# 512-column values for heads 2 and 3, attentions queued ahead of their Q and K, longer holds, and another pace of the side sums

## The chip, the cores and the metric

The kernel runs on one core of a Trainium2 chip. TensorE (PE) does the matmuls, VectorE (DVE), ScalarE (ACT) and GpSimd (POOL) the elementwise work, SyncE (SP) issues the loads and stores. Each engine works through its own queue in order, and waits where an operand is not there yet. The metric is the time of one execution on the device in microseconds; a profiled execution gives a trace of what each engine did and waited for.

## The reference

One encoder layer on x of 1024 tokens by 1024 channels, in float32:

```python
h = rmsnorm(x, norm_mix)
q, k, v, r, lr_f, lr_b, u, g_a, g_b = split(h @ w_in)
log_a_f = log_sigmoid(lr_f @ w_decay_up_fwd + b_decay_fwd) / 16    # and log_a_b
# 4 heads, keys of 128, values of 256, in chunks of 64, forward and backward:
#   b = cumsum(log_a) within the chunk;  q_e = q exp(b);  k_e = k exp(-b)
#   scores = masked q_e k_e^T;  kv = k_d^T v;  state = decay * state + kv
#   o = scores v + q_e state
o = rms(o_fwd + o_bwd) per head * gla_norm * silu(r)
y_a = o @ w_branch_gla
y_b = (pooled mixer of u) @ w_pool_group * pool_scale
x = x + (sigmoid(g_a) * y_a + sigmoid(g_b) * y_b) @ w_out
x = x + (silu(gate) * up) @ w_ffn_out      # of rmsnorm(x) @ w_ffn_in
out = rmsnorm(x, norm_final)
```

What the change touches is the first projection, q, k and v of the four heads, and the attention that follows for each head.

## The kernel before

Every float32 operand of a product is split in two parts, a rounded one and the rest (`split_to`: ScalarE copies, VectorE or POOL subtracts), and one product is three matmuls: high by high, high by low, low by high (`products`). `mm3` is one such product; a bank of PSUM holds 512 columns of float32, and eight products over the 1024 channels (KT = 8 blocks of 128) fill it. Weights come by `load` as raw tiles (four buffers), which `Weights.split` turns into wh and wl (ScalarE casts, POOL subtracts; six buffers each).

The program writes the order of all engines itself (a manual schedule). The stream of projection products on TensorE sets the pace. After each product, `pump` counts its width in units of 512 columns and lets other work have its turn: `pending` (splits of the next weights, one for each two units), `aside` (sums that are prepared for later stages: branch sums of the GLA output weight, wsum tiles on POOL; later feature sums on VectorE and POOL; each step followed by a number of units, the pace), and `side`. In `side` stand the attentions, Python generators that are run one after the other: each issues some steps, then yields the number of units until its next ones. So the work of one head's attention is spread among the projection products of the next head.

An attention begins with four decay stages (two halves of the tokens, two directions; names by tile): z, a matmul for the decay's logits, la and z on VectorE and ScalarE (abs, exp, ln), a scan on VectorE with tot and z behind it, the exponentials on ScalarE (qe, z, fac), then ke on VectorE, qe and fac on POOL. HOLD is the number of units between one of these stages and the next. The transposed keys follow (kp on TensorE, kt on ScalarE and VectorE), then seven state steps for the backward direction: kv on TensorE, st on VectorE, sb and so on ScalarE, where so is what the next st adds to. Then the scores (sc on TensorE, masked on VectorE, split into p), and for each block of tokens the output op. When the head is done, its o is normalised on VectorE (`unscaled`, run by the next attention behind its z stage) and stored by SP (o_out).

The main loop does Q and K of a head (`project_qk`, each two banks of 512 tokens), and then begins the head's attention. Values of heads 0 and 1 are made at once, 512 columns a bank (`pair_products`, in the stage of head 0). Those of heads 2 and 3 are made by head: `values` fills 256 columns of a bank for each of eight blocks of tokens, from weights that `Weights` splits.

Of the kernel before, what the change touches and what calls it, by code (L numbers as in the profile page):

```python
# [10 lines left out]
F32 = mybir.dt.float32  # L11
F32R = mybir.dt.float32r
# [41 lines left out]
def kernel(  # L54
# [42 lines left out]
    def slot(dtype=F32, shape=(2, HALF), s="slot"):  # L97
        return slots.tile([P, *shape], dtype, tag="slot", name=name(s))
# [10 lines left out]
    def bank(pool, s="ps"):  # L109
        return pool.tile([P, HALF], F32, tag=pool.name, name=name(s))  # L110
# [88 lines left out]
    def split_to(hi, lo, src, eng=nc.vector):  # L199
        nc.scalar.copy(hi, src)  # L200
        eng.tensor_tensor(lo, src, as_f32(hi), op=ALU.subtract)  # L201
# [92 lines left out]
    def tokens(pair, t):  # L294
        return tuple(p[:, (t % 4) * P : (t % 4 + 1) * P] for p in pair)
# [138 lines left out]
    def low_rank_weights():  # L434
# [7 lines left out]
    def value_slots():  # L442
        return [(slot(F32R, (4, DV), "vh"), slot(F32R, (4, DV), "vl")) for _ in range(2)]

    cols = const.tile([P, 40], F32, tag="cols", name="cols")

# [41 lines left out]
    split_pair_weight()  # L488
    for kp in range(2):
        transpose_tile(trs[kp], xn[1], 1, kp)  # L490
    pair_v = [[], []]

    def pair_products(ts, before=None):
        banks = [bank(ps_mm) for _ in ts]
        for k in range(KT):
            if before:
                before(k)
            for ps, t in zip(banks, ts):
                mm3(ps[:, :], tokens(hT(k, t // 4), t), pair_w[k], k == 0, k == KT - 1)
        for ps, t in zip(banks, ts):  # L500
            for h in range(2):
                if t // 4 == len(pair_v[h]):
                    pair_v[h].append((slot(F32R, (4, DV), "vh"), slot(F32R, (4, DV), "vl")))
            parts = [[part[:, t % 4, :] for part in v[t // 4]] for v in pair_v]
            halves = [ps[:, h * DV : (h + 1) * DV] for h in range(2)]
            for (hi, _), src in zip(parts, halves):
                nc.scalar.copy(hi, src)
            for (hi, lo), src in zip(parts, halves):
                nc.vector.tensor_tensor(lo, src, as_f32(hi), op=ALU.subtract)

    def first_steps(k):
        if k == 2:
# [211 lines left out]
            aside.pop(0)  # L724


    v_heads, o_heads, unscaled = {}, {}, []
    HOLD, SCORES = 4.4, 6

    def project_qk():  # L730
# [7 lines left out]
        return q, k  # L738

    def attention(h, q, k):  # L740


        qe, ke = {}, {}
# [139 lines left out]
        kts[0, 1] = transposed_keys(0, 1)  # L883
        exponentials(1, 0)
        yield 2.5
        while h not in v_heads:
            yield 0.5
        v = v_heads[h]

        def value(n):  # L890
            return tuple(part[:, n % 4, :] for part in v[n // 4])
# [12 lines left out]
        p = scores(0)  # L904
        yield SCORES
        o = [slot(shape=(4, DV), s="o") for _ in range(2)]
        ms = vec(NT, "oms")
        old = sf = None
# [50 lines left out]
    def first_qk():  # L959
        q, k = slot(s="q"), slot(s="k")  # L960
        low_rank(0)
        weights = [take()]
        for half in range(2):
            if half:
                finish_side()
                low_rank(1)
                prepare()
            for n, (dst, scale) in enumerate(((q, DK**-0.5), (k, 1.0))):
                if n == len(weights):
                    weights.append(take(ahead=False))  # L970
                ps = feature_major(weights[n], hT, half)
                nc.scalar.activation(dst[:, half, :], ps[:, :], AF.Copy, scale=scale)
        return q, k

    for h in range(HEADS):
        qk = project_qk() if h else first_qk()
        begin(attention(h, *qk))
        if h == 0:
            for ts in ((7,), (6,), (5, 4)):
                pair_products(ts)  # L980
            v_heads.update(enumerate(pair_v))
            prepare_beside(map(branch_jobs, range(4)), 5)
        if h > 1:
            v = value_slots()
            w = take()
            for t in range(NT):
                values(w, v, t)
            v_heads[h] = v

    class Unit:  # L990

# [131 lines left out]
    for j in range(KT):  # L1123
        if 2 <= j <= 4:
            load_o(j - 2)
        w = take()
        if j == 6:
            for _ in range(2):
                gunits[0].load()
        if j == 7:  # L1130
            gates_ahead.step()
        if j < BY:
            whole_r = slot(s="r")
        for half in range(2):
# [898 lines left out]
```

## Time and profile before

| | before |
|---|---|
| time, median of 3 runs | 1379.94 us (1379.63 to 1380.65) |
| profiled execution | 1380.1 us |
| its span, first to last instruction | 1378.1 us |
| granted TensorE clock | 0.999 |
| busy TensorE / weight loads | 1367.6 us (99%) / 1147.4 us (83%) |
| busy VectorE / ScalarE / POOL | 61% / 47% / 54% |
| value matmuls of heads 2 and 3 | 384 of 128x256 |

Names in the rows are tiles, out<-in, with buffer numbers left out; L274 is the line of `products`, so that nearly all projection and state matmuls stand on one line and are told apart by tiles: ps for a projection bank, kv, op, sc and kp for an attention. Matmuls overlap, and the duration of one says how long it was on its way; how many microseconds it takes of TensorE is seen from the distance between two starts. What stands in brackets is the idle time of the engine before the instruction and what ended it.

The attention of head 1 (counted from 0) lies beside Q and K of head 2 and the values of head 2, from about 132 us in the span on; that of head 2 beside Q and K of head 3 and its values, that of head 3 beside the R columns.

### The profile page before, as it was taken

How to read it: one execution, taken by the hardware profiler on the slowest of the kernel's cores; microseconds unless marked ns; L12 is line 12 of the kernel's file. 1: busy time of each engine (PE TensorE's matmuls, PEld its weight loads, DVE VectorE, ACT ScalarE, POOL GpSimd, SP SyncE). 2: the span in 40 equal slices, each digit the busy share in tenths (PEclk: the TensorE clock that was granted, in tenths of full speed). 3: DMA queues.
4: the chain of work that ended last, by engine and by line, in shares of the span. 5: the costliest groups of instructions: out<-in, count | busy, mean ns of one | idle time of the engine just before them, and what ended most of it. 6: DMA issues, size and time to landing. Idle time of an engine off the chain costs nothing. (4 is left out here: it accounts for less than half of the span.)

```text
span 1378.1 us, 18207 instructions
## 1 busy us (share of the span) xinstructions
PE 1367.6 (99%) x6514; PEld 1147.4 (83%) x6514; DVE 839.8 (61%) x1027; ACT 642.6 (47%) x1170; POOL 750.7 (54%) x554
## 2 busy tenths in 40 slices
PE   9999999999999999999999999999999999999998
PEld 7888899988888888888888888888888888888886
DVE  6364656557745876688883955656656556343375
ACT  7375666655334445554347533333333334444353
POOL 3222617132297646668665276666666667455454
PEclk9999999999999999999999999999999999999999
DMA  6121413312478678996516355555544447985561
GB/s 226 31 62 47 147 62 125 110 48 77 138 230 278 197 229 277 371 394 216 175 61 245 115 176 176 176 176 176 165 143 139 144 136 266 385 306 186 170 214 77
DMA packets 166586, 243.60 MB, mean 177 GB/s; under 512 B 10936, under 2 KB 95968, under 8 KB 166496
## 3 DMA queue, kind: packets, MB, share of 16 engines
q1 hardware_dynamic: 166352, 242.18, 52.3%
q8 instruction: 51, 0.84, 0.3%
q14 instruction: 39, 0.32, 0.1%
q10 hardware_dynamic: 144, 0.26, 0.1%
HBM read 164.55 MB, written 77.86 MB: 176 GB/s over the span
## 5 line engine op out<-in xcount | busy, mean ns | idle before, releaser
L201 POOL TENSOR_TENSOR wl<-fs,wh 128x512 fp32r<-128x512 f32 x120 | 167.6, 1400 | 157.2 <-ACT wh L200 103.2
L274 PE MATMUL ps<-gh,wh 128*128 128x512 f32 x616 | 240.9, 391 | 0.0
L274 PE MATMUL ps<-gl,wh 128*128 128x512 f32 x616 | 240.2, 390 | 0.3 <-DVE gl L1591 0.3
L274 PE MATMUL ps<-gh,wl 128*128 128x512 f32 x616 | 240.0, 390 | 0.0
L201 POOL TENSOR_TENSOR wl<-fraw,wh 128x512 fp32r<-128x512 f32 x90 | 129.7, 1441 | 63.6 <-ACT wh L200 61.2
L274 PE MATMUL ps<-hh,wh 128*128 128x512 f32 x376 | 151.9, 404 | 0.0
L201 POOL TENSOR_TENSOR ol<-gor,oh 128x1024 fp32r<-128x1024 f32 (+1 forms) x42 | 101.7, 2425 | 85.7 <-ACT oh L200 59.6
L274 PE MATMUL ps<-hh,wl 128*128 128x512 f32 x376 | 146.9, 391 | 0.0
L274 PE MATMUL ps<-hl,wh 128*128 128x512 f32 x376 | 146.8, 390 | 0.0
L274 PEld LDWEIGHTS ps<-gl,wh 128*128 128x128 f32 x616 | 115.8, 188 | 24.1 <-DVE gl L1591 0.7
L274 PEld LDWEIGHTS ps<-gh,wh 128*128 128x128 f32 x616 | 115.8, 188 | 24.0 <-ACT hb L1610 0.3
L274 PEld LDWEIGHTS ps<-gh,wl 128*128 128x128 f32 x616 | 115.7, 188 | 24.1
L201 POOL TENSOR_TENSOR wl<-raw,wh 128x512 fp32r<-128x512 f32 x40 | 54.7, 1379 | 121.9 <-ACT wh L200 103.5
L274 PE MATMUL ps<-oh,oh 128*128 128x512 f32 x308 | 120.0, 390 | 0.0
L274 PE MATMUL ps<-oh,ol 128*128 128x512 f32 x308 | 120.0, 390 | 0.0
L274 PE MATMUL ps<-ol,oh 128*128 128x512 f32 x308 | 120.0, 389 | 0.0
L201 POOL TENSOR_TENSOR wl<-wraw,wh 128x512 fp32r<-128x512 f32 x56 | 92.2, 1675 | 44.7 <-ACT wh L200 44.5
L201 DVE TENSOR_TENSOR ol<-wor,oh 128x1024 fp32r<-128x1024 f32 (+1 forms) x42 | 62.8, 1506 | 68.1 <-ACT oh L200 55.5
L200 ACT CAST wh<-fs 128x512 fp32r<-128x512 f32 x120 | 73.8, 615 | 26.1 <-DVE fs L1010 25.1
L274 PEld LDWEIGHTS ps<-hh,wl 128*128 128x128 f32 x376 | 70.6, 188 | 15.0
L274 PEld LDWEIGHTS ps<-hl,wh 128*128 128x128 f32 x376 | 70.9, 188 | 12.9
L274 PEld LDWEIGHTS ps<-hh,wh 128*128 128x128 f32 x376 | 70.8, 188 | 12.8
(279 smaller groups left out, 3126.3 us busy)
## 6 DMA issues: line engine op xcount, KB each, us to landing
fraw<-in_w_ffn_in_dram SPq DMA_DIRECT2D x44, 512.0 KB, 7.2
gor<-g_out SPq DMA_DIRECT2D x35, 512.0 KB, 5.8
g_out<-s SPq DMA_DIRECT2D x44, 256.0 KB, 2.3
raw<-in_w_in_dram SPq DMA_DIRECT2D x40, 256.0 KB, 5.1
fraw<-in_w_in_dram SPq DMA_DIRECT2D x20, 512.0 KB, 7.1
wor<-t_out SPq DMA_DIRECT2D x20, 512.0 KB, 4.5
g_out<-g SPq DMA_DIRECT2D x33, 256.0 KB, 2.5
x<-in_x_dram SPq DMA_DIRECT2D x16, 512.0 KB, 4.5
```

The lines of the kernel that those rows point to most:

```text
L200: nc.scalar.copy(hi, src)
L201: eng.tensor_tensor(lo, src, as_f32(hi), op=ALU.subtract)
L274: nc.tensor.matmul(ps, a[i], b[j], start=first and n == 0, stop=last and n == 2, skip_group_check=onto)
```

## The change

Five things are changed.

1. The values of heads 2 and 3 are made together, 512 columns a bank, in one stage behind Q and K of head 2, by a new class `ValueWeights`. It loads the eight weight blocks of 128 rows by 512 columns, takes them in the order 0, 1, 6, 7, 2, 3, 4, 5 (6 and 7 into slots of their own), and does the token blocks 7 and 6 first, in two banks: the first six weights for both, then the last two for both. Then come blocks 5 to 0. `values` and `value_slots` go; the splitting of a bank into both heads is shared with heads 0 and 1 (`keep_values`). Q and K of head 3 come behind it.
2. The attention of head h + 1 is put into `side` before its Q and K are projected. It begins when the one before has ended, and waits (in steps of half a unit) for `qk_heads` where it first needs q and k, and before each state step for the value tile of that step.
3. HOLD goes from 4.4 to 5.0.
4. A step of the branch sums is followed by 4.5 units and not 5.
5. A step of the feature sums is followed by 2.8 units and not 2.3.

```diff
-        cols_of = [(Q0 + h * DK, DK), (K0 + h * DK, DK), (V0 + h * DV, DV)]
-        order += [(w_in, KT, *c) for c in cols_of[: 2 if h < 2 else 3]]
+        order += [(w_in, KT, c + h * DK, DK) for c in (Q0, K0)]
...
-    def values(w, v, t):
-        ps = bank(ps_mm)
-        for kt in range(KT):
-            mm3(ps[:, :DV], tokens(hT(kt, t // 4), t), w(kt), kt == 0, kt == KT - 1)
-        split_to(*(part[:, t % 4, :] for part in v[t // 4]), ps[:, :DV])
...
+    def keep_values(heads, t, ps):
+        vs = [v_slots[h] for h in heads]
+        for v in vs:
+            if t // 4 not in v:
+                v[t // 4] = slot(F32R, (4, DV), "vh"), slot(F32R, (4, DV), "vl")
+        parts = [[part[:, t % 4, :] for part in v[t // 4]] for v in vs]
+        for h in heads:
+            v_tiles[h].add(t)
+        halves = [ps[:, h * DV : (h + 1) * DV] for h in range(2)]
+        for (hi, _), src in zip(parts, halves):
+            nc.scalar.copy(hi, src)
+        for (hi, lo), src in zip(parts, halves):
+            nc.vector.tensor_tensor(lo, src, as_f32(hi), op=ALU.subtract)
...
-            prepare_beside(map(branch_jobs, range(4)), 5)
-        if h > 1:
-            v = value_slots()
-            w = take()
-            for t in range(NT):
-                values(w, v, t)
-            v_heads[h] = v
+            prepare_beside(map(branch_jobs, range(4)), 4.5)
+        if h == 2:
+            value_weights.pop().products()
...
-    HOLD, SCORES = 4.4, 6
+    HOLD, SCORES = 5.0, 6
...
+    class ValueWeights:
+        ORDER = (0, 1, 6, 7, 2, 3, 4, 5)
+        IN_SLOTS = (6, 7)
...
+        def load(self, upto):
+            while len(self.raw) < min(upto, KT):
+                k = self.ORDER[len(self.raw)]
+                raw = wts.tile([P, HALF], F32, tag="raw", name=name("raw"), bufs=4)
+                nc.sync.dma_start(raw[:, :], w_in[k * P : (k + 1) * P, V0 + 2 * DV : V0 + 4 * DV])
+                self.raw.append(raw)
...
+                    mm3(banks[t][:, :], tokens(hT(k, t // 4), t), self.parts[k], at == 0, at == KT - 1)
+                if ks[-1] == self.ORDER[-1]:
+                    keep_values((2, 3), t, banks[t])
+
+            early, late = self.ORDER[:6], self.ORDER[6:]
+            for ks in (early, late):
+                for t in (7, 6):
+                    steps(t, ks)
+            for t in reversed(range(NT - 2)):
+                if t == 2:
+                    fetch()
+                steps(t, self.ORDER)
...
+        while h not in qk_heads:
+            yield 0.5
+        q, k = qk_heads[h]
         apply_decay(1, 1)
...
+            while n not in v_tiles[h]:
+                yield 0.5
             old = advance(old, n, 1, kts[n // 4, 1], sb[m // 4][:, m % 4, :], m == 0)
...
-        qk = project_qk() if h else first_qk()
-        begin(attention(h, *qk))
+        if h:
+            project_qk(h, h == 2)
+        else:
+            first_qk()
+            begin(attention(0))
+        if h < HEADS - 1:
+            begin(attention(h + 1))
...
-                prepare_beside([feature_jobs(0), feature_jobs(1)], 2.3)
+                prepare_beside([feature_jobs(0), feature_jobs(1)], 2.8)
```

On TensorE, where the values of head 2 began before (ps_1633 is their bank; hh and hl are parts of h, kp and kv belong to the attention of head 1):

```order
L274 MATMUL ps_1633<-wh_1518,hh_223 128x256
L274 MATMUL ps_1633<-wl_1519,hh_223 128x256
L274 MATMUL ps_1633<-wh_1518,hl_224 128x256
L826 MATMUL kp_1637<-ident,ke_1584 128x128 x4
L274 MATMUL ps_1633<-wh_1518,hh_223 128x256
L274 MATMUL ps_1633<-wl_1519,hh_223 128x256
L274 MATMUL ps_1633<-wh_1518,hl_224 128x256
```

and the same place now, where ps_1650 is a bank for both heads:

```order
L273 MATMUL ps_1650<-wh_1466,hh_494 128x512
L273 MATMUL ps_1650<-wl_1467,hh_494 128x512
L273 MATMUL ps_1650<-wh_1466,hl_495 128x512
L885 MATMUL kp_1654<-ident,ke_1596 128x128 x4
L273 MATMUL ps_1650<-wh_1480,hh_494 128x512
L273 MATMUL ps_1650<-wl_1481,hh_494 128x512
L273 MATMUL ps_1650<-wh_1480,hl_495 128x512
```

Matmuls of 256 columns became matmuls of twice the width, and the transposes kp of head 1's attention stand at the same place in the stage.

On SP's queue, before, the store of head 0's normalised output (o_out) and the loads of the value weights of head 2 (raw_1497 to raw_1503) behind it; wsum and s_out are loads and stores of the branch sums:

```order
L687 DMA s_out_542<-wsum_1051 128x512
L604 DMA wsum_1452<-in_w_branch_gla_dram 128x2x512
L604 DMA wsum_1453<-in_w_branch_gla_dram 128x2x512
L570 DMA o_out_561<-o_1164 128x1024
L570 DMA o_out_561<-o_1165 128x1024
L687 DMA s_out_541<-wsum_1050 128x512
L208 DMA raw_1497<-in_w_in_dram 128x2x256
L208 DMA raw_1499<-in_w_in_dram 128x2x256
L208 DMA raw_1501<-in_w_in_dram 128x2x256
L208 DMA raw_1503<-in_w_in_dram 128x2x256
```

and now (the raw tiles are the value weights of both heads, one block of 128 rows each):

```order
L738 DMA raw_1397<-in_w_in_dram 128x512
L738 DMA raw_1399<-in_w_in_dram 128x512
L563 DMA o_out_561<-o_1177 128x1024
L563 DMA o_out_561<-o_1178 128x1024
L738 DMA raw_1462<-in_w_in_dram 128x512
L738 DMA raw_1464<-in_w_in_dram 128x512
L738 DMA raw_1478<-in_w_in_dram 128x512
L738 DMA raw_1490<-in_w_in_dram 128x512
L738 DMA raw_1501<-in_w_in_dram 128x512
L680 DMA s_out_542<-wsum_1028 128x512
L597 DMA wsum_1506<-in_w_branch_gla_dram 128x2x512
L597 DMA wsum_1507<-in_w_branch_gla_dram 128x2x512
```

Two of the value weights are now loaded ahead of o_out and five directly behind it; the second pair of wsum loads moved from ahead of o_out to behind them.

On ScalarE, the casts of the value weights and the first exponentials of head 1's decays (qe, z and fac), before:

```order
L737 ACTIVATE q_1379<-ps_1385 128x512
L764 ACT_TABLE_LOAD
L764 ACTIVATE z_1389<-z_1389 128x512
L764 ACTIVATE z_1397<-z_1397 128x512
L764 ACTIVATE z_1405<-z_1405 128x512
L764 ACTIVATE z_1417<-z_1417 128x512
L737 ACTIVATE q_1379<-ps_1458 128x512
L200 CAST wh_1518<-raw_1497 128x512
L798 ACT_TABLE_LOAD
L798 ACTIVATE qe_1522<-z_1389 128x512
```

and now:

```order
L823 ACTIVATE z_1413<-z_1413 128x512
L200 CAST wh_1466<-raw_1397 128x512
L796 ACTIVATE q_1391<-ps_1401 128x512
L200 CAST wh_1480<-raw_1399 128x512
L200 CAST wv_1492<-raw_1462 128x512
L200 CAST wv_1503<-raw_1464 128x512
L796 ACTIVATE q_1391<-ps_1471 128x512
L200 CAST wh_1535<-raw_1478 128x512
L857 ACT_TABLE_LOAD
L857 ACTIVATE qe_1542<-z_1372 128x512
```

Before, one cast of a value weight loaded behind o_out stood ahead of the exponentials; now there are three of them (raw_1462, raw_1464, raw_1478), and two of weights loaded earlier.

More of the change, by code (lines that the diff above doesn't have):

```diff
@@ L440, in low_rank_weights @@
         nc.vector.tensor_tensor(up[32:64], uraw[32:64], as_f32(up[32:64]), op=ALU.subtract)
-    def value_slots():
-        return [(slot(F32R, (4, DV), "vh"), slot(F32R, (4, DV), "vl")) for _ in range(2)]
     cols = const.tile([P, 40], F32, tag="cols", name="cols")
@@ L490 @@
         transpose_tile(trs[kp], xn[1], 1, kp)
-    pair_v = [[], []]
+    v_slots, v_tiles, qk_heads = [{} for _ in range(HEADS)], [set() for _ in range(HEADS)], {}
+    def keep_values(heads, t, ps):
[11 more added lines that the diff above has]
+            nc.vector.tensor_tensor(lo, src, as_f32(hi), op=ALU.subtract)
     def pair_products(ts, before=None):
@@ L500, in pair_products @@
         for ps, t in zip(banks, ts):
[L501 to L509, printed above, removed]
+            keep_values((0, 1), t, ps)
     def first_steps(k):
@@ L724, in finish_beside, with __init__, split, splits @@
             aside.pop(0)
-    v_heads, o_heads, unscaled = {}, {}, []
-    HOLD, SCORES = 4.4, 6
-    def project_qk():
+    o_heads, unscaled = {}, []
+    HOLD, SCORES = 5.0, 6
+    class ValueWeights:
+        ORDER = (0, 1, 6, 7, 2, 3, 4, 5)
+        IN_SLOTS = (6, 7)
+        def __init__(self):
+            self.raw, self.parts = [], {}
+            self.load(2)
+            self.splits(4)
+        def load(self, upto):
[4 more added lines that the diff above has]
+                self.raw.append(raw)
+        def split(self):
+            n = len(self.parts)
+            self.load(n + 4)
+            k = self.ORDER[n]
+            if k in self.IN_SLOTS:
+                w = slot(F32R, s="wv")
+                parts = w[:, 0, :], w[:, 1, :]
+            else:
+                parts = [wts.tile([P, HALF], F32R, tag=s, name=name(s))[:, :] for s in ("wh", "wl")]
+            split_to(*parts, self.raw[n][:, :], nc.gpsimd)
+            self.parts[k] = parts
+        def splits(self, n):
+            pending.extend([self.split] * n)
+        def products(self):
+            while pending:
+                pending.pop(0)()
+            banks = {}
+            self.split()
+            self.split()
+            def steps(t, ks):
+                if t not in banks:
+                    banks[t] = bank(ps_mm)
+                for k in ks:
+                    if (t, k) == (0, 6):
+                        prepare()
+                        credit[0] = 1.0
+                    at = self.ORDER.index(k)
+                    mm3(banks[t][:, :], tokens(hT(k, t // 4), t), self.parts[k], at == 0, at == KT - 1)
[9 more added lines that the diff above has]
+                steps(t, self.ORDER)
+    def project_qk(h, last=False):
         q = slot(s="q")
@@ L733, in project_qk @@
         for dst, scale in ((q, DK**-0.5), (k, 1.0)):
-            w = take()
+            final = last and dst is k
+            w = take(not final)
+            if final:
+                value_weights[0].splits(2)
+            elif last:
+                value_weights.append(ValueWeights())
             for half in range(2):
@@ L737, in project_qk, with attention @@
                 nc.scalar.activation(dst[:, half, :], ps[:, :], AF.Copy, scale=scale)
-        return q, k
-    def attention(h, q, k):
+        qk_heads[h] = q, k
+    def attention(h):
         qe, ke = {}, {}
@@ L885, in attention @@
         yield 2.5
-        while h not in v_heads:
-            yield 0.5
-        v = v_heads[h]
         def value(n):
-            return tuple(part[:, n % 4, :] for part in v[n // 4])
+            return tuple(part[:, n % 4, :] for part in v_slots[h][n // 4])
         sb = [slot(shape=(4, DV), s="sb") for _ in range(2)]
@@ L905, in attention @@
         yield SCORES
+        while 0 not in v_tiles[h]:
+            yield 0.5
         o = [slot(shape=(4, DV), s="o") for _ in range(2)]
```

6 lines of the change are left out of this document (3 added, 3 removed).

## The prediction

> **What bounds the kernel now.** I read the page's busy shares first, then the chain that ended last, then the groups of the value matmuls kept apart by shape.
>
> ```profile
> PE 1367.6 (99%) x6514; PEld 1147.4 (83%) x6514; DVE 839.8 (61%) x1027; ACT 642.6 (47%) x1170; POOL 750.7 (54%) x554
> PE 44%; DVE 1%; ACT 1%; issue 0%; POOLq 0%; POOL 0%; DVEq 0%; ACTq 0%
> L274 PE MATMUL ps<-wh,hh 128*128 128x256 f32 x128 | 40.0, 312 | 0.0
> L274 PE MATMUL ps<-wh,hl 128*128 128x256 f32 x128 | 36.2, 283 | 0.0
> L274 PE MATMUL ps<-wl,hh 128*128 128x256 f32 x128 | 36.2, 283 | 0.0
> ```
>
> TensorE is the bound; the rest of the chain is small. So the change is worth what it takes from TensorE's stream of matmuls and from the gaps in it. The last three rows are the 384 value matmuls of heads 2 and 3. Their mean is not what they cost: the busy column holds overlapping matmuls. The cost of one is its distance from the next, which the timeline of TensorE shows, first in a value stage (256 columns), then in a Q/K or R stage (512):
>
> ```profile
> 232.38 0.28 PE L274 MATMUL ps<-wh,hl 128*128 128x256 f32 x1
> ...
> 235.97 0.28 PE L274 MATMUL ps<-wh,hl 128*128 128x256 f32 x1
> 273.27 0.39 PE L274 MATMUL ps<-hh,wl 128*128 128x512 f32 x1
> ...
> 274.86 0.39 PE L274 MATMUL ps<-hh,wh 128*128 128x512 f32 x1
> ```
>
> There are 30 starts from the first row to the second: 3.59/30 = 0.120 us each. There are 7 from the third to the fourth: 1.59/7 = 0.227 us.
>
> The gaps come next. Here are TensorE's rows around the attention of head 1 (which runs in the value stage of head 2), with one row of head 3's:
>
> ```profile
> 154.53 0.28 PE L274 MATMUL ps<-wh,hl 128*128 128x256 f32 x1
> 155.29 0.66 PE L826 MATMUL kp<-ident,ke 128*128 128x128 f32 x4 [0.49 <-DVE ke L808]
> ...
> 157.58 0.28 PE L274 MATMUL kv<-vh,kt 128*128 128x256 f32 x1
> ...
> 168.82 1.16 PE L856 MATMUL sc<-qe,ke 128*128 128x128 f32 x8 [0.24 <-DVE st L840]
> ...
> 175.08 0.39 PE L274 MATMUL op<-vh,p 128*128 128x256 f32 x1 [0.22 <-DVE p L201]
> ...
> 298.82 0.39 PE L274 MATMUL op<-vh,p 128*128 128x256 f32 x1 [0.22 <-DVE p L201]
> ```
>
> The kp matmuls begin 0.76 us after the one before them, where 0.12 is the pitch: 0.64 lost, of which the idle column shows 0.49 (the ends of matmuls are modelled). Adding the same 0.15 to the other idles, head 1's attention loses about 0.64 + 0.39 + 0.37 = 1.4 us and head 3's 0.37. VectorE explains them:
>
> ```profile
> 135.65 5.31 DVE L943 TENSOR_SCALAR o<-o,ors 128x256 f32<-128x256 f32 x8
> ...
> 154.56 0.68 DVE L808 TENSOR_TENSOR ke<-z,k 128x512 f32<-128x512 f32 x1
> ...
> 161.22 0.47 DVE L838 TENSOR_SCALAR st<-kv,fac 128x256 f32<-128x256 f32 x1
> ...
> 165.36 0.48 DVE L840 SCALAR_TENSOR_TENSOR st<-kv,fac,so 128x256 f32<-128x256 f32 x1 [0.98 <-ACT so L848]
> 166.82 0.48 DVE L840 SCALAR_TENSOR_TENSOR st<-kv,fac,so 128x256 f32<-128x256 f32 x1 [0.98 <-ACT so L848]
> ```
>
> The first state update st starts at 161.22, 3.6 us behind the first kv at 157.58, because VectorE is still at the decays. Then the updates follow each other at 166.82 - 165.36 = 1.46 us (st, then ScalarE's so, then st), so a late start is never made up, and kv, sc and p come late in turn. In head 2's attention the same distance is smaller:
>
> ```profile
> 220.99 0.28 PE L274 MATMUL kv<-vh,kt 128*128 128x256 f32 x1
> 223.36 0.47 DVE L838 TENSOR_SCALAR st<-kv,fac 128x256 f32<-128x256 f32 x1
> ```
>
> 2.4 us, and TensorE's waits list no gap there. So what counts is the lateness beyond some 2.4 us. Why head 1 is so late, ScalarE and SP's queue show:
>
> ```profile
> 147.88 0.62 ACT L200 CAST wh<-raw 128x512 fp32r<-128x512 f32 x1 [4.14 <-DMA raw<-in_w_in_dram]
> 138.90 2.42 SPq L570 DMA_DIRECT2D o_out<-o  x2
> ...
> 141.91 2.73 SPq L208 DMA_DIRECT2D raw<-in_w_in_dram  x4
> ```
>
> SP sends o_out only once VectorE's normalisation (135.65, above) has written o, and the value weights' loads stand behind it. ScalarE takes the cast of those weights before the exponentials of the decays, and idles 4.14 us.
>
> **The change, part by part.** *Values of heads 2 and 3.* Out: 384 matmuls at 0.120 us. In: 192 at 0.227. 46.1 - 43.6 = **-2.5 us** on TensorE, which is the path. 192 weight loads go too, and they lie beside matmuls. The Trainium skill, "TensorE: Matmul & The Clock Gate", section "Wait — 56ns, not 53.3ns?", puts the fixed cost of a matmul at about 2.5 ns once warm, which would make this term only 192 x 2.5 ns = 0.5 us (an estimate from that page). The rows here give 240 - 227 = 13 ns, and the sum takes them. The ScalarE casts and VectorE subtractions of the values stay as many and as wide (vh, vl, 256 columns): nothing.
>
> *Head 1's attention: the longer holds and the earlier queueing.* HOLD stands four times between decays and first kv, 0.6 units more each; a unit is one 512-column product of three matmuls, 3 x 0.227 = 0.68 us. So VectorE and ScalarE have 4 x 0.6 x 0.68 = 1.6 us more. The attention also begins its z matmuls before the Q stage of head 2 and not within it, so that the holds cost no later kv on TensorE. The normalisation and o_out come up to 2 us earlier with it, the value loads behind them too: ScalarE's cast still waits, but shorter. Lateness 3.6 - 1.6 = 2.0, less whatever the earlier loads give: under 2.4. The gaps before kp and sc go (1.0 us); I leave 0.2 of that before p (0.37), since the first two value banks now end right there with two casts and two subtractions each. **-1.2 us**; the ends are 0 and -1.4.
>
> *Head 3's attention.* It has the same 1.6 us and no values beside its decays: **-0.4**; the ends are 0 and -0.4.
>
> *Head 2's attention.* It pays. Its decays now run in the long value stage and not in Q and K of head 3, so that VectorE has two subtractions more for each bank of 8 x 0.68 = 5.4 us:
>
> ```profile
> L201 DVE TENSOR_TENSOR vl<-ps,vh 128x256 fp32r<-128x256 f32 x16 | 6.6, 421 | 13.1 <-ACT vh L200 13.1
> ```
>
> Its four decay stages and their holds take some 4 x 5.0 x 0.68 = 13.6 us, in which 2.5 banks end: 2.5 x 2 x 0.42 = 2.1 us of VectorE, against the 1.6 us that the holds give. Lateness 2.4 + 2.1 - 1.6 = 2.9, half a microsecond past the point from which it costs; some of the subtractions fall into VectorE's idle time. **+0.3**; the ends are 0 and +0.9 (1.4 us is what 3.6 us of lateness cost; a good half of it).
>
> *Queues that are passed.* On SP, four more value loads now go out behind o_out and before the second pair of branch loads (wsum). On POOL the subtractions for the value weights of k = 4 and 5 stand behind four wsum operations, three qe products and three fac products. Their prices:
>
> ```profile
> L706 POOL TENSOR_TENSOR wsum<-wsum 128x512 f32<-128x512 f32 x16 | 22.4, 1403 | 0.6 <-DMA wsum<-in_w_branch_gla_dram 0.2
> L809 POOL TENSOR_TENSOR qe<-qe,q 128x512 f32<-128x512 f32 x16 | 23.6, 1473 | 28.2 <-ACT qe L798 27.8
> wsum<-in_w_branch_gla_dram SPq DMA_DIRECT2D x8, 512.0 KB, 6.5
> ```
>
> If wsum is issued at some 143.5 (o_out up to 2 us earlier, five loads at 2.73/4 us behind it) it lands at 150; 4 x 1.4 + 3 x 1.5 + 3 x 0.5 = 11.6 us later POOL is at the two weights, and has them at 164.5 (1.4 us each). TensorE reads the first of them 8 products, 7 kv (3 x 0.12 each) and one kp after the first kv: 5.4 + 2.5 + 0.5 = 8.4 us after 157.6, at 166. Hidden by 1.5 us; past that each microsecond is one of TensorE's. The weights of Q in head 3 are split in the value stage, with more room: nothing.
>
> *Branch sums at 4.5 instead of 5, feature sums at 2.8 instead of 2.3.* They run on POOL, VectorE and DMA while TensorE does R and Q/K. The feature sums begin at the fourth or fifth of eight R columns; a column is 2 x 8 products, 10.9 us. Some 25 steps at 2.8 x 0.68 = 1.9 us take 48 us, 8.5 more than at 2.3 (25 x 0.5 x 0.68), and four to five columns last 44 to 55. In the changed program's order the last feature step stands about a dozen products (8 us) ahead of the gates that need it, so I put them at nothing; without that cover, up to those 8.5 us.
>
> Sum: -2.5 - 1.2 - 0.4 + 0.3 = -3.8. The profiled execution took 1380.1 (span 1378.1 and 2.0 around it): 1376.3. It stands 0.2 above the median of the three runs: **1376.0** with rounding.
>
> **The rivals.** *All gaps go, and head 2 pays nothing:* -2.5 - 1.4 - 0.4, and small gaps of a tenth that I did not count go along (perhaps 1 us): 1374.6. For it speaks that lateness under 2.4 us showed no gap at all; against it head 2's subtractions.
>
> *The gaps stay; only the wider matmuls count* (the holds do not do what they are for): 1379.9 - 2.5 + 0.3 = 1377.7. For it: ScalarE's cast waited for a load, not for the pace of the holds, and the casts that now precede the exponentials are three, of the first, second and third load behind o_out, where it was one. If the loads are no earlier than 141.91, the third goes out 1.4 us behind the first and two casts of 0.6 us stand before it: the exponentials are then some 2 us later than in the profile, kp's gap goes from 0.6 to 2.6 us, and the sum is 1380.
>
> *A pair of narrow matmuls costs hardly more than a wide one:* the values give next to nothing of the 2.5, at the least 0.5 us, and the sum is -0.5 - 1.2 - 0.4 + 0.3 = -1.8, 1378.0, inside 0.2%. For it: nothing in the rows; against it: 30 starts in a row at 0.120. The page of the Trainium skill named above is what would have it so.
>
> *Slower: the same casts, with the loads later still.* ScalarE's queue is in order, so the exponentials of both directions, ke, kp, kv and with them TensorE stand behind the third load. The values give 2.5 and the other terms nothing, so that the time passes 1382.7 (slower by 0.2%) once this load comes some 5 us later than the 147.88 of the profile: at 1 us of gap for each beyond, 6 us later would be 1383.7. For it: two kinds of loads and the o_out store share one queue, and a wsum load took 6.5 us. Against it: o_out goes out earlier, not later, and the loads behind it are as wide as before.
>
> *The busy column is the cost:* 112.4 us go and 192 x 0.39 = 74.9 come: 1342. The pitch of 0.120 and 0.227 excludes it nearly.
>
> **How the numbers follow.** Two per mille (2.8 us) is about what a measurement of this kernel tells from no change. The forecast 0.42, all gaps gone 0.14, gaps stay 0.21, narrow pair as good as a wide one 0.03, slower 0.18, busy column 0.02. Faster 0.42 + 0.14 + 0.02 = 0.58; same 0.21 + 0.03 = 0.24; slower 0.18. The range runs from 1373.0 (the first rival with as much again for uncounted gaps) to 1383.0 (past the edge of "slower", with the case of late loads begun); some 0.05 lie below and 0.13 above. The likeliest case alone: 1374.6 to 1377.7, by the ends of its terms.
>
> **What would show it.** Right: TensorE has 192 matmuls fewer, the value matmuls are 128x512 with 0.227 us between starts; the idle before kp and sc in head 1's attention is gone; the first st follows the first kv by less than 2.4 us in heads 1 and 3; the profile's waits list at most a small gap in head 2's attention. Wrong: ScalarE idles over 4 us on a raw load as before, or kp waits for ke by more than 0.5 us; a wait of a value matmul for a POOL wl in the first two banks; a wait at the start of the gates for feature sums. If the pitch of the 512-column value matmuls is not 0.227, the first term falls.

## The result

The changed kernel took 1377.07 us (median, 1376.69 to 1377.90), the kernel before 1379.65 us in the same measurement (1379.15 to 1380.65): a ratio of 0.9982, 95% interval 0.9974 to 0.9990. That is 2.6 us faster, where 3.9 were forecast; the range and the direction held.

The page of the changed kernel, its span and its busy shares:

```profile
span 1375.0 us, 17836 instructions
PE 1364.8 (99%) x6322; PEld 1135.8 (83%) x6322; DVE 834.0 (61%) x1027; ACT 642.6 (47%) x1170; POOL 749.4 (55%) x554
```

192 matmuls are gone (6514 before), and the span is 3.1 us shorter than in the profile before (1378.1). TensorE is still the bound. Its rows in head 1's attention, in the places that were quoted of before:

```profile
155.04 0.39 PE L273 MATMUL ps<-wh,hl 128*128 128x512 f32 x1
155.27 0.60 PE L885 MATMUL kp<-ident,ke 128*128 128x128 f32 x4
...
157.56 0.39 PE L273 MATMUL ps<-wv,hl 128*128 128x512 f32 x1
157.78 0.28 PE L273 MATMUL kv<-vh,kt 128*128 128x256 f32 x1
...
166.26 0.39 PE L273 MATMUL ps<-wh,hh 128*128 128x512 f32 x1
166.95 0.50 PE L273 MATMUL ps<-wl,hh 128*128 128x512 f32 x1 [0.30 <-POOL wl L201]
...
173.83 0.38 PE L273 MATMUL op<-vh,p 128*128 128x256 f32 x1 [0.28 <-ACT p L200]
...
174.56 0.39 PE L273 MATMUL op<-vh,p 128*128 128x256 f32 x1 [0.23 <-DVE p L201]
```

The kp matmuls start 0.23 us behind the one before them, where they started 0.76 behind: that gap is gone, and so is the one before sc. A value matmul (157.56) is 0.22 us ahead of the next instruction. Two gaps are left: one for p, as before, and a new one of 0.69 - 0.23 = 0.46 us, for the low part of a value weight that POOL has not made yet.

How late the first state update is, in heads 1, 2 and 3 (TensorE's first kv, then VectorE):

```profile
157.78 0.28 PE L273 MATMUL kv<-vh,kt 128*128 128x256 f32 x1
160.27 0.47 DVE L897 TENSOR_SCALAR st<-kv,fac 128x256 f32<-128x256 f32 x1
...
221.98 0.28 PE L273 MATMUL kv<-vh,kt 128*128 128x256 f32 x1
224.55 0.76 DVE L492 TENSOR_TENSOR vl<-ps,vh 128x256 fp32r<-128x256 f32 x2 [1.22 <-ACT vh L490]
225.22 0.47 DVE L897 TENSOR_SCALAR st<-kv,fac 128x256 f32<-128x256 f32 x1
...
285.13 0.28 PE L273 MATMUL kv<-vh,kt 128*128 128x256 f32 x1
285.68 0.48 DVE L897 TENSOR_SCALAR st<-kv,fac 128x256 f32<-128x256 f32 x1
```

2.5, 3.2 and 0.55 us, where it was 3.6, 2.4 and 3.3. In head 2 VectorE idles 1.22 us for ScalarE's copies of a value bank (vh), because the bank's end was put into the order just ahead of the first st. I read that as a price of order: the values now end beside these decays.

ScalarE's wait, POOL's wait and SP's queue in head 1's decays:

```profile
146.44 0.62 ACT L200 CAST wh<-raw 128x512 fp32r<-128x512 f32 x1 [1.58 <-DMA raw<-in_w_in_dram]
148.38 0.60 ACT L857 ACTIVATE qe<-z 128x512 f32<-128x512 f32 x1
...
155.46 1.30 POOL L699 TENSOR_TENSOR wsum<-wsum 128x512 f32<-128x512 f32 x1 [4.01 <-DMA wsum<-in_w_branch_gla_dram]
...
165.60 2.54 POOL L201 TENSOR_TENSOR wl<-raw,wh 128x512 fp32r<-128x512 f32 x2
138.25 9.23 SPq L738 DMA_DIRECT2D raw<-in_w_in_dram  x5
...
148.11 0.99 SPq L597 DMA_DIRECT2D wsum<-in_w_branch_gla_dram  x2
```

ScalarE now waits 1.58 us for a raw tile and not 4.14, and its first exponential (qe) comes at 148.38, where it came at 149.82. But SP takes 9.23 us over the five loads, where four took 2.73 before. The program has four raw buffers, and a load waits for one to be free: in the trace the last four of the five go out at 139.83, 143.72, 144.98 and 147.14, each within 0.03 us of the end of a POOL subtraction that read a raw tile. So wsum goes out only at 148.1, and POOL stands 4.01 us before it, with the two value weights behind (165.60).

The same wait reaches p. POOL has no idle time from 155.46 until its last qe product of head 1 ends, at 169.36, and ScalarE's copy of the third tile of transposed keys (kt) starts 0.03 us later:

```profile
168.08 1.28 POOL L868 TENSOR_TENSOR qe<-qe,q 128x512 f32<-128x512 f32 x1
169.39 0.59 ACT L200 CAST kt<-kp 128x512 fp32r<-128x512 f32 x1 [1.69 <-POOL qe L868]
170.01 0.69 DVE L201 TENSOR_TENSOR kt<-kp,kt 128x512 fp32r<-128x512 f32 x1 [3.25 <-ACT kt L200]
```

The kp that it copies was done by 164.3. As I read it, kt takes a buffer that the qe product still reads; no run took that apart. VectorE idles 3.25 us for kt, and the last two state updates, the mask of the scores and p stand behind it in VectorE's order.

### The profile page after: what moved, and what is told of

The parts are those of the page before. It is cut to its first block, busy times and chain, and to the rows that moved or that the text cites. A ratio compares the mean times of both kernels' runs of the same rounds, so it can differ in the third digit from the quotient of the medians.

```text
span 1375.0 us, 17836 instructions
## 1 busy us (share of the span) xinstructions
PE 1364.8 (99%) x6322; PEld 1135.8 (83%) x6322; DVE 834.0 (61%) x1027; ACT 642.6 (47%) x1170; POOL 749.4 (55%) x554
```

## The experiments

Gaps below are counted from the trace's starts: a matmul that starts over 0.06 us later behind the one before it than the median for the same sequence of tiles and shapes; they are summed for the attention of each head. What the profile's waits show as idle is less, since the ends of matmuls are modelled. The first two rows of the table are the kernel before and the changed one; the others are told below. Ratios, with 95% interval, are to the kernel before as measured beside each, where its median was 1379.5 to 1379.9 us; they compare better than the medians. The intervals of narrow, paces_old, scores7, scores_12, mixed and p_later overlap that of the changed kernel.

Spans and gaps are those of one profiled execution each, and one order does not give the same gaps every time: up to the outputs of head 1 the changed kernel and p_later have the same order, and TensorE loses 0.57 us (0.46 and 0.11, over two starts) to POOL's value weight in the one and 0.95 in the other. A difference of 0.4 us between two rows is not yet an effect.

| kernel | median us | ratio | span us | gaps in heads 0, 1, 2, 3 | span less gaps |
|---|---|---|---|---|---|
| before | 1379.65 | | 1378.1 | 0, 2.6, 0, 1.0 | 1374.5 |
| changed | 1377.07 | 0.9982 (0.9974 to 0.9990) | 1375.0 | 0.3, 1.6, 0.6, 0 | 1372.5 |
| values_alone | 1384.11 | 1.0033 (1.0020 to 1.0045) | 1382.3 | 0, 4.3, 3.4, 1.9 | 1372.7 |
| before_hold5 | 1378.93 | 0.9995 (0.9986 to 1.0004) | 1377.4 | 0.3, 2.2, 0.1, 0 | 1374.8 |
| narrow | 1378.94 | 0.9995 (0.9986 to 1.0004) | 1377.2 | 0.3, 1.6, 0.6, 0 | 1374.7 |
| hold44 | 1381.31 | 1.0013 (1.0005 to 1.0022) | 1379.5 | 0, 2.4, 4.5, 0 | 1372.6 |
| late_begin | 1379.61 | 1.0001 (0.9992 to 1.0009) | 1378.3 | 0.3, 3.1, 1.2, 1.3 | 1372.4 |
| paces_old | 1377.75 | 0.9985 (0.9976 to 0.9994) | 1375.9 | 0.3, 1.5, 1.2, 0 | 1372.9 |
| scores7 | 1378.24 | 0.9989 (0.9980 to 0.9998) | 1376.2 | 0.3, 1.5, 0.5, 1.1 | 1372.7 |
| hold56 | 1383.45 | 1.0029 (1.0018 to 1.0040) | 1381.0 | 0, 7.1, 0, 1.0 | 1372.9 |
| head0_44 | 1379.52 | 1.0000 (0.9992 to 1.0009) | 1377.0 | 0, 2.9, 1.7, 0 | 1372.4 |
| scores_12 | 1378.29 | 0.9991 (0.9982 to 1.0000) | 1375.7 | 0.3, 0.5, 2.4, 0 | 1372.4 |
| mixed | 1378.81 | 0.9994 (0.9986 to 1.0003) | 1377.0 | 0, 3.7, 1.0, 0 | 1372.4 |
| p_later | 1376.19 | 0.9975 (0.9966 to 0.9985) | 1374.1 | 0.3, 1.3, 0, 0 | 1372.5 |

The last column is the main finding. Whatever the holds, paces and queueing, the span less its gaps is 1372.4 to 1372.9 with 512-column values (eleven kernels) and 1374.5 to 1374.8 with 256-column ones (three). In hold56 the 7.1 us of head 1 hold some time at a lower clock behind its long wait (last section). So the wide values are worth about 2.1 us, and all else that the change does is a matter of gaps.

### The wide values alone

The changed kernel with everything but the values put back:

```diff
-    HOLD, SCORES = 5.0, 6
+    HOLD, SCORES = 4.4, 6
...
-            prepare_beside(map(branch_jobs, range(4)), 4.5)
+            prepare_beside(map(branch_jobs, range(4)), 5)
...
         if h:
             project_qk(h, h == 2)
         else:
             first_qk()
-            begin(attention(0))
-        if h < HEADS - 1:
-            begin(attention(h + 1))
+        begin(attention(h))
...
-                prepare_beside([feature_jobs(0), feature_jobs(1)], 2.8)
+                prepare_beside([feature_jobs(0), feature_jobs(1)], 2.3)
```

> The 512-column values of heads 2 and 3 alone, in one stage behind Q and K of head 2; HOLD 4.4, the attentions begun behind their Q and K, branch and feature sums at 5 and 2.3 as before. Theory (the pitch of the value matmuls gives 2.3 us, and the attentions lose what they lost before or a little more, since head 2's decays now lie beside the values): 1377.3 to 1378.6, with the gaps at kp and p of head 1 still in the trace. Rival (the gain of the whole change is the holds' and the queueing's, the wider matmuls give next to nothing): 1379.2 or more.

1384.11 us, 4.3 slower than the kernel before beside it (1379.85). The theory missed it; the rival's open end (1379.2 or more) holds the number, but not for its reason, since the matmuls save here what they save in the other kernels. The gaps are 9.6 us, 6.0 more than before's. Among TensorE's waits (total, times, longest):

```profile
PE op L984 <- ACT sf L903: 2.4, 3, 1.7
...
PE kp L885 <- DVE ke L867: 0.8, 1, 0.8
```

The wide values bring head 2's decays and the end of head 1 among casts of value banks, and move Q and K of head 3 with head 3's attention back: its last outputs run into the activation table load of the R columns (1.9 us of gap there). So the wide values cost more than they give, unless the rest of the change is made too.

### The longer holds in the kernel before

```diff
-    HOLD, SCORES = 4.4, 6
+    HOLD, SCORES = 5.0, 6
```

> The kernel before with HOLD 5.0 and nothing else. Theory (VectorE's lateness at the first state update is what costs, and a longer hold takes it away wherever the attention is queued): the gap at kp and those of head 3 go, about 1.5 to 2 us: 1377.7 to 1378.2. Rival (the cast that waits 4.1 us for the value weights holds head 1's decays, so that longer holds alone move only head 3): 1.0 us, 1378.7.

1378.93 us, 0.9 less than the kernel before beside it (1379.85), and 1.0 by the gaps: near the rival's 1.0, though the interval of the ratio still includes no change. Head 3's gaps are gone, as both had it. In head 1 the gap at kp went and two others came; its first st still starts 3.6 us after the first kv, for the reason that the rival gave. TensorE's waits list, as the longest of the new ones:

```profile
PE ps L274 <- POOL wl L201: 0.6, 2, 0.4
```

### The changed kernel with narrow values

```diff
-                    mm3(banks[t][:, :], tokens(hT(k, t // 4), t), self.parts[k], at == 0, at == KT - 1)
+                    for c in (0, DV):
+                        half = [p[:, c : c + DV] for p in self.parts[k]]
+                        mm3(banks[t][:, c : c + DV], tokens(hT(k, t // 4), t), half, at == 0, at == KT - 1, True)
```

The two halves of a bank are accumulated in turns here, and the values of heads 2 and 3 do not come out as the reference's; instructions and shapes are those of 256 columns.

> The changed kernel, but each value product of heads 2 and 3 as two of 256 columns into the two halves of the bank, in the same stage: 192 matmuls more, everything else as in the changed kernel. Theory (0.240 us for two narrow ones, 0.227 for a wide one): 2.3 to 2.5 us more than the changed kernel, about 1379.4. Rival (a pair of narrow ones costs hardly more than a wide one): 0.5 us more, 1377.6.

1378.94 us, 1.9 more than the changed kernel; by the spans of the profiles, at gaps that agree to 0.1 us, 2.2. Each of its 11 spans (1376.5 to 1378.5) lies above each of the changed kernel's 15 (1374.6 to 1375.8). The pitch read from the rows is borne out (13 ns for each of 192 pairs would be 2.5), and the 0.5 us by the rule that the prediction took from the Trainium skill ("TensorE: Matmul & The Clock Gate", section "Wait — 56ns, not 53.3ns?") does not agree with the spans.

### The old hold in the changed kernel

```diff
-    HOLD, SCORES = 5.0, 6
+    HOLD, SCORES = 4.4, 6
```

> The changed kernel with HOLD 4.4. Theory (each hold's 0.6 units are 1.6 us of lateness in each attention): the first st lags the first kv by about 4.1 us in head 1 (2.5 in the changed kernel), the gaps of heads 1 and 2 grow by 1 to 1.5 us each and those of head 3 come back with 1 us, head 0's gap of 0.3 goes: 1379.5 to 1380.5. Rival (queueing ahead suffices, the longer holds give nothing): 1377.1.

1381.31 us, 4.2 more than the changed kernel; the theory had the sign and fell 0.8 short of the size. It also placed it wrongly: head 1's first st lags by 2.95 us and not by 4.1, head 3 shows no gap, head 1 0.8 us more, and head 2 4.0 more. In head 2 VectorE comes to the second key product just after a value bank's subtractions:

```profile
214.49 0.76 DVE L492 TENSOR_TENSOR vl<-ps,vh 128x256 fp32r<-128x256 f32 x2
215.16 0.68 DVE L867 TENSOR_TENSOR ke<-z,k 128x512 f32<-128x512 f32 x1
...
215.90 0.33 PE L885 MATMUL kp<-ident,ke 128*128 128x128 f32 x1 [1.11 <-DVE ke L867]
```

That wait is 1.3 us by starts; the first st of head 2 then lags by 4.8 us, and kv, sc and p wait in turn for the rest. So the 0.6 units are worth 0.9 us in the kernel before and 4.2 here: they are what makes room for the values beside the decays.

### The attentions queued behind their Q and K

```diff
         if h:
             project_qk(h, h == 2)
         else:
             first_qk()
-            begin(attention(0))
-        if h < HEADS - 1:
-            begin(attention(h + 1))
+        begin(attention(h))
```

> The changed kernel, but each attention is begun behind its own Q and K, as before. Theory (with HOLD 5.0 alone the kernel before kept 2.2 us of gaps in head 1, and here the values lie beside head 2's decays too; queueing ahead brings z forward by some 2 units): head 1's first st lags by 3.5 us and more, gaps of heads 1 and 2 grow by 1 to 2 us in all: 1378.2 to 1379.2. Rival (queueing ahead gives nothing, the holds are all): 1377.1.

1379.61 us, 2.5 more than the changed kernel, somewhat over the theory. Head 1's lateness is hardly larger (2.6 us against 2.5), so that part was wrong; its value matmul waits 0.9 us and not 0.3 for POOL, and its p another 0.6 longer. Head 2 has 0.6 us more, so that the gaps of heads 1 and 2 together grew by the 2 us of the theory, and 1.3 us came at the end of head 3's attention, as in the run with more time for p below.

### The old paces of the side sums

```diff
-            prepare_beside(map(branch_jobs, range(4)), 4.5)
+            prepare_beside(map(branch_jobs, range(4)), 5)
...
-                prepare_beside([feature_jobs(0), feature_jobs(1)], 2.8)
+                prepare_beside([feature_jobs(0), feature_jobs(1)], 2.3)
```

> The changed kernel with the old paces, branch sums every 5 units and feature sums every 2.3. Theory (the paces only shift work of POOL, VectorE and ScalarE that lies beside TensorE): within 0.7 us of the changed kernel, 1376.6 to 1377.8; the 0.6 us that a value matmul waits for POOL may go or double, since a wsum operation that waits for its load stands ahead of it. Rival (the faster branch sums carry part of the gain): 1379 or more, with a gap that was not there.

1377.75 us, within what the theory allowed, and by the gaps 0.6 more than the changed kernel. The value matmul no longer waits for POOL, since two of the four wsum operations now stand behind the two subtractions, which begin at 162.72 and not at 165.60. ScalarE's copy of kt no longer waits for POOL (it starts at 167.28, not at 169.39), and p of head 1 does not keep TensorE waiting either. In their place gaps of 1.0 and 0.5 us came among head 1's outputs, and head 2's grew.

### More time for p, in all heads

```diff
-    HOLD, SCORES = 5.0, 6
+    HOLD, SCORES = 5.0, 7
```

> The changed kernel with 7 units and not 6 between the scores and the first output op. Theory (p is late by 1.0 us in head 1 and 0.6 in head 2 because the chain of state updates is, and one unit is 0.68 us): 0.5 to 1.1 us less than the changed kernel, about 1376.2. Rival (the attentions become too long, and what ends later runs into the next one's decays): 1377.5 or more.

1378.24 us: the rival. The gaps at p are gone in heads 1 and 2, and as much came elsewhere in the same heads. The attentions follow each other, so a unit for each head adds up, and head 3's outputs now meet ScalarE's table load and gates of the R columns:

```profile
317.65 1.28 ACT L1160 ACT_TABLE_LOAD   x1
318.94 0.63 ACT L1160 ACTIVATE sr<-r 128x512 f32<-128x512 f32 x1
319.48 0.58 ACT L1160 ACTIVATE sr<-ps 128x512 f32<-128x512 f32 x1
321.45 0.51 ACT L903 ACTIVATE sf<-st,fac 128x256 f32<-128x256 f32 x1 [1.39 <-DVE st L899]
```

TensorE waits 0.9 us for that sf. The theory's ground was also not the one at work in head 1: the last two state updates there wait for kt, as the rows of the changed kernel show.

### Longer holds still

```diff
-    HOLD, SCORES = 5.0, 6
+    HOLD, SCORES = 5.6, 6
```

> The changed kernel with HOLD 5.6. Theory (lateness falls by another 1.6 us, to 0.9 in head 1 and 1.6 in head 2): the gaps at p go, 1.0 to 1.5 us less, 1375.6 to 1376.2. Rival (there is a point past which longer holds push the end of an attention into the next stage, as the gap of 0.3 us at the end of head 0's attention, which came with HOLD 5.0, begins to show): more gaps there and in head 3, 1377.5 to 1379.

1383.45 us: slower, as the rival had it, but far beyond its numbers and in another place (head 0's gap is gone, and head 3 has 1.0 us). The lateness fell as the theory had it (0.6 and 0.8 us), and head 2 has no gap. But p of head 1 keeps TensorE waiting for 3.8 us:

```profile
161.61 10.87 SPq L680 DMA_DIRECT2D s_out<-wsum  x4
...
174.67 0.76 DVE L492 TENSOR_TENSOR vl<-ps,vh 128x256 fp32r<-128x256 f32 x2 [3.95 <-DMA s_out<-wsum]
175.34 0.48 DVE L899 SCALAR_TENSOR_TENSOR st<-kv,fac,so 128x256 f32<-128x256 f32 x1
...
180.42 0.58 PE L273 MATMUL op<-vh,p 128*128 128x256 f32 x1 [3.80 <-ACT p L200]
```

The low part of the values (vl) takes a buffer from which a branch sum is still to be stored; VectorE waits for that store, the store stands on SP behind POOL's sums, and st and p stand behind vl on VectorE. In the changed kernel VectorE shows no such wait at this place.

### Shifting one head, or two

HOLD 4.4 for head 0 alone:

> The changed kernel with HOLD 4.4 for head 0 alone, 5.0 for the others. Theory (head 0 had no gap with 4.4, and the attentions follow each other, so that all of head 1's decays come some 2 us earlier against Q and K of head 2): head 0's gap of 0.3 us goes, head 1's lateness falls below 2.5 and part of its 1.0 us at p goes: 1376.0 to 1376.8. Rival (each shift meets other work of POOL and the loads, so that a gap appears for each that goes): 1377.1 or more.

7 units behind the scores in heads 1 and 2, HOLD 4.6 in head 3:

> The changed kernel with 7 units between scores and outputs in heads 1 and 2 alone, and HOLD 4.6 in head 3. Theory (p's gaps of 1.0 and 0.6 us go with the extra unit; head 3 pays its extra 1.4 us of delay back in its holds and stays clear of the activation table load of the gates): 1375.5 to 1376.3, no gap in head 3. Rival (as above, new gaps for old): 1377.1 or more.

HOLD 4.4 for head 0, and 7 units in head 2:

> HOLD 4.4 for head 0, 5.0 for the others, and 7 units behind the scores in head 2 alone. Theory (both steps add up): head 0's gap and head 2's gap at p go, 0.9 us, and part of head 1's: 1375.6 to 1376.4. Rival: 1377.1 or more.

The edit is the same in all three, with other numbers:

```diff
-    HOLD, SCORES = 5.0, 6
+    HOLDS, WAITS = (4.4, 5.0, 5.0, 5.0), (6, 6, 6, 6)
...
-        yield HOLD
+        yield HOLDS[h]
...
-        yield SCORES
+        yield WAITS[h]
```

1379.52, 1378.29 and 1378.81 us: the rival three times, new gaps for old. Part of what was meant came: head 0's gap is gone in the first and third, p's in scores_12's head 1 is down to a third, and head 3 has no gap. But 0.5 us at p of head 2 stayed in the second and third, and each moved everything behind it. In scores_12, for one, head 2's first st comes 5.2 us after its kv, behind a late value bank once more:

```profile
226.12 0.76 DVE L492 TENSOR_TENSOR vl<-ps,vh 128x256 fp32r<-128x256 f32 x2 [1.22 <-ACT vh L490]
226.79 0.47 DVE L897 TENSOR_SCALAR st<-kv,fac 128x256 f32<-128x256 f32 x1
```

### More time for p, with nothing behind it moved

```diff
-        yield SCORES
+        yield SCORES + (h in (1, 2))
...
-            yield 1.02
+            yield 0.895 if h in (1, 2) else 1.02
         rs = rms_scale(ms[:, :], NT, "ors")
```

> The changed kernel with one unit more between the scores and the outputs in heads 1 and 2, and an eighth of a unit less behind each of the eight token blocks that follow, so that the next head's decays and everything behind stand where they stood in the order. Theory (p is late there because the chain of state updates is, and nothing else hangs on it): the gaps at p of 1.0 and 0.6 us shrink to 0.4 or less each, no gap comes in their place, span 1373.8 to 1374.3, 1375.8 to 1376.4. Rival (the outputs then run into a wait that p's gap covered, as the extra unit did that moved all behind it): span 1375.0 and 1377.1 again, or more.

1376.19 us, 0.9975 of the kernel before (0.9966 to 0.9985): the fastest of all, with the span that the theory gave. The wait for p is gone from the list; at its place 0.4 us are left in head 1 and none in head 2. The one for POOL's weight is longer, although nothing ahead of it was changed: wsum came 0.3 us later in this execution.

```profile
PE ps L273 <- POOL wl L201: 0.9, 2, 0.7
```

It and the changed kernel were measured apart, each beside the kernel before; the intervals of the two ratios overlap, and the spans differ by 0.9 us (medians of all spans 1374.1 and 1375.0).

The theory's ground needs a correction. Head 1's first st lags by only 1.6 us in this execution, and p is no earlier for it: kt waits 2.92 us for POOL's qe product, and p comes 0.3 us later than in the changed kernel. The extra unit covers that wait; it does not cover lateness of the first st.

## Why the prediction was right, and where it was off

By direction and range the forecast held, though 2.6 us lies just inside the two per mille (2.8 us) at which the prediction drew its own line for no change. The forecast of 1376.0 was 1.1 us low; the sum of its terms was -3.8 against -3.1 in the spans of the two profiles and -2.6 in the medians. The profile before that was used stood 0.45 us above the median of the larger set of runs, and not 0.2: that is part of the difference.

- *Values, -2.5.* Right in kind, a little too large: 2.1 by the spans less gaps, 2.2 by the narrow kernel. The rival in which a pair of narrow matmuls costs as much as a wide one is out.
- *Head 1, -1.2.* -1.0 (2.6 to 1.6 us of gaps), of other parts. The gaps at kp and sc went as said. The prediction counted 1.4 us there, from idle times, where the starts give 2.6, so a gain of nearly the forecast size came out of a loss almost twice as large. The lateness fell to 2.5 us and not below 2.4, and p's gap did not shrink at all: by starts it was 0.8 us and is 1.0, where 0.2 was allowed. Its cause changed: before, VectorE reached kt with 0.12 us of idle time; now it idles 3.25 us for kt, which waits for POOL. And 2.4 us of lateness is no threshold: in head0_44 and mixed head 2's first st lags by 2.2 us, and that head has 1.7 and 1.0 us of gaps.
- *The queue on POOL, "hidden by 1.5 us".* This step failed, and a wait of a value matmul for a POOL wl was one of the prediction's own signs of being wrong: TensorE lost 0.6 us there, and 1.0 at p through kt, a way that the prediction did not have. The chain to the weights was the right one, the size was not: the loads ahead of wsum were taken at 2.73/4 us each, and SP needed 9.23 us for five, since each waited for POOL to free a raw buffer. wsum landed at 155.5 and not at 150. With two of the four wsum operations behind the weights (paces_old) both waits are gone.
- *Head 2, +0.3.* +0.6, by starts, and by another way than counted: an order in which a value bank ends between kt and st.
- *Head 3, -0.4.* -1.0. The term was sized from one row of the gap at p; the gaps that the kernel before had at sc were not counted.
- *Head 0* was overlooked: the hold is longer there too, and its last outputs wait 0.3 us for ScalarE's sf.
- *The side sums, nothing.* The old paces cost 0.6 us of other gaps, so they were not free of effect: the branch sums' pace decides how many wsum operations stand ahead of the value weights on POOL, which the prediction did not connect.

The forecast was made of separate terms, and the runs do not bear that out. The values alone cost 4.3 us, the longer holds gave 0.9 in the kernel before and 4.2 in the changed one, the queueing ahead 2.5. The rival "the gaps stay; only the wider matmuls count" was priced at 1377.7, and by its number it was nearer (0.6 us off) than the forecast. Its ground is out, since the gaps at kp and sc are gone; and the kernel in which only the values are wide took 1384.1: with other positions the gaps do not stay. The total came out near in part by luck: by the terms, the errors were +0.4 (values), +0.2 (head 1), +0.3 (head 2), +0.3 (head 0) and -0.6 (head 3). That holds, paces and positions had been fitted to each other, as I read it, the profile of before could not show. The slower rival is out too: the exponentials came 1.4 us earlier, not later.

## What to carry to other kernels

Where one engine is full, count its gaps by starts and hold the span less the gaps against a variant's: here that split every result into what the matmuls cost (two values, 2.1 us apart) and what the order cost. In a static order with one queue of side work, a longer or shorter step moves everything behind it; of six attempts to close a gap in the changed kernel, only the one gained (0.9 us by the spans) that gave the time back within the same head. A wait is to be followed back to its first cause: here one late load on SP's queue showed as a wait for a weight and as a wait for p. A change that widens matmuls moves the casts at the ends of banks with it, and is to be measured together with the pace of the work beside it.

## What the runs showed of the hardware

When TensorE had idled 3.8 us (in hold56), it ran at a lower granted clock for the next microseconds. The columns are busy time of each engine in the stretch, then the granted clock and the share of DMA:

```profile
176.00:180.00 4.00, 0.61 (x3) 0.19 (x1) 1.84 (x4) 2.02 (x6) 0.00 (x0) 1.00 0.00 0
180.00:184.00 4.00, 3.58 (x14) 3.03 (x15) 1.60 (x3) 1.38 (x4) 0.00 (x0) 0.57 0.00 0
184.00:188.00 4.00, 4.00 (x28) 3.68 (x27) 1.55 (x3) 2.39 (x9) 0.00 (x0) 1.00 0.00 0
```

14 matmuls in the second stretch against 28 in the third. Shorter waits left no such trace: behind the longest of values_alone (1.67 us, for sf) the granted clock stayed at 1.00.

VectorE's scan and POOL's products held each other up. At the same place of the same order, POOL's qe product began 0.16 us ahead of the scan in the changed kernel, and 0.14 us behind it in p_later:

```profile
156.72 1.29 POOL L868 TENSOR_TENSOR qe<-qe,q 128x512 f32<-128x512 f32 x1
156.88 2.22 DVE L837 TENSOR_TENSOR_SCAN z<-carry,la 128x512 f32<-128x512 bf16 x1
157.97 1.12 POOL L869 TENSOR_TENSOR fac<-fac 128x4 f32<-128x4 f32 x1
```

```profile
156.91 1.27 DVE L837 TENSOR_TENSOR_SCAN z<-carry,la 128x512 f32<-128x512 bf16 x1
157.05 2.21 POOL L868 TENSOR_TENSOR qe<-qe,q 128x512 f32<-128x512 f32 x1
159.23 0.19 POOL L869 TENSOR_TENSOR fac<-fac 128x4 f32<-128x4 f32 x1
```

The one that began first took 1.29 or 1.27 us, and the other about 0.9 us longer than that. POOL's tiny fac product took 1.12 us beside the scan and 0.19 without it. This is why head 1's first st lags by 2.5 us in the one and by 1.6 in the other, with nothing ahead of it changed. In hold44 the scan of the same shape took 1.23 us where POOL was idle:

```profile
218.15 1.23 DVE L837 TENSOR_TENSOR_SCAN z<-carry,la 128x512 f32<-128x512 bf16 x1
...
220.77 1.29 POOL L868 TENSOR_TENSOR qe<-qe,q 128x512 f32<-128x512 f32 x1 [2.88 <-ACT qe L857]
```

Not all work of VectorE does this: in scores_12 a fac product took 0.20 us at 226.27, while VectorE was at the subtraction vl that began at 226.12. All this is read from such rows; no run took it apart.
